# The first weight piece in two halves on two queues, into accumulators set to zero, and the second weight tile requested behind the norm's weights

## The chip, the cores and the metric

The kernel runs on one core of a Trainium2 chip. The metric is the device time of one execution in microseconds (us). The core has a matrix engine (TensorE; PE in the profile, its weight loads PEld), VectorE (DVE), ScalarE (ACT), GpSimd (POOL), SyncE (SP, which mostly issues DMAs here) and 16 DMA engines that serve all queues.

## The reference

One layer of an encoder on 256 positions of width 2048, all in float32. A first norm (RMS norm with the gain `g_mix_pre`) feeds one combined projection `w_in` of 2048 x 5120; attention, a recurrent branch, an output projection, a feed-forward block and a per-layer gate follow. The change touches only the beginning:

```
h = x
hn = rms_norm(h, g_mix_pre[i])
u = hn @ w_in[i]
q, k, v, xr, yg = jnp.split(u, [D_ATTN, 2 * D_ATTN, 3 * D_ATTN, 3 * D_ATTN + D_REC], axis=-1)
```

## The kernel before, in words

Every large product is made of three matmuls. Each float32 operand is split into a high part in the reduced format fp32r (what a cast to it leaves) and a low part (the rest), and the product is high x high + low x high + high x low. The activations are the stationary operand, in blocks of 128 x 128; the weights stream past in 512 columns. A weight tile is 256 rows x 512 columns, kept as two row blocks of 128 x 512 (256 KB each). For each tile a DMA on the SP queue fills a raw buffer `wr` (L611, one of four), ACT casts it to the high part `wh` (L699), VectorE subtracts to make the low part `wl` (L715), and `products` (L730) issues the matmuls: two halves of the positions (t0, t1) x three matmuls x two row blocks, 12 for a tile.

The norm is folded in: the activations are x, transposed, times the gain (`make_hT`, L964): ACT makes the high part `hT_hi` (L330), VectorE the low part `hT_lo` (L332). The gain's 8 KB, `g_first`, are the one load on the ACT queue (L303). The blocks of x come as `xs` (L946) on the SP queue, in between the weights. The scale by row is applied to the result later.

The first three tiles are loaded, cast and subtracted in two pieces of one row block each (`pieces`, L569, with `EARLY`). For tile 0 `products` has an order of its own: first the four matmuls that need the high part alone (L741, L742), then the two with the low part (L755). All later tiles go half by half of the positions through L753, L754 and L755. The first matmul into an accumulator carries a start flag and overwrites it; the others add.

Tiles 0 and 1 take the same rows of `w_in` for two column chunks with two accumulators each; tiles 2 and 3 take the next rows for the same chunks, and so on. On SP the order at the start is: x block 0, tile 0 first piece, x block 1, tile 0 second piece, tile 1 first piece, tile 1 second piece, x blocks 2 and 3, tile 2 in two pieces, tile 3, x blocks 4 and 5. Tile 4 needs the raw buffer of tile 0, so its request waits until VectorE has made the last low part of tile 0.

Before the first segment the program issues a copy on ACT that brings in its function table (L2251) and a warm-up of TensorE: `WARM` = 9 matmuls of a 128x128 float32 tile of ones, two instructions each in the trace (L2254).

The order of the work on ACT, VectorE and SP is not written by hand. A planner (`Plan`) keeps a clock for each engine, with costs written in the code (`act`, `dve`, `dma`; `MM` = 0.2263 for one matmul of 512 columns, `SEM` = 0.15 for a handover), and issues the next operation whose start plus lateness is least, before TensorE's clock reaches it (`plan.run`). `plan.main` advances TensorE's clock for the matmuls. In microseconds of the planner, `dve(n)` is 0.08 + 0.00104 n. For tile 0's first piece the planner counts:

```
plan.main(4 * MM, ev_hi[p], lhs.ev[kx + j])
...
plan.main(2 * MM, ev_lo[p])
```

Of the kernel before, what the change touches and what calls it, by code (L numbers as in the profile page):

```python
# [16 lines left out]
P = 128  # L17
# [71 lines left out]
ADDED = 6.0  # L89
AHEAD = 5  # L90
ISSUE = 160
WARM = 9


class Event:
# [141 lines left out]
def act(n, tables=COPY, take=None, give=None):  # L237
    return ("act", COST["act"] + 0.00082 * n, tables, take, give)
# [15 lines left out]
def layer(ctx: ExitStack, tc: tile.TileContext, a: dict, out: bass.AP):  # L254
# [7 lines left out]
    def f32(t):  # L262
        return t.bitcast(F32)
# [6 lines left out]
    def raw_tile(i):  # L270
        if i not in more_raws:
            return wp.tile([P, 2, N], F32, tag="wr", name="wr", bufs=R_BUFS)
        return t2["third"]
# [4 lines left out]
    def w_kind(i):  # L278
        return f"w{more_w[i]}" if i in more_w else "w"

    def w_tiles(i):
        if i not in more_w:
            return [wp.tile([P, 2, N], F32R, tag=t, name=t) for t in ("wh", "wl")]
        if "w" not in t2:
            t2["w"] = t2["pool"].tile([P, 4, N], F32R, tag="gain", name="w")
        return t2["w"][:, 0:2, :], t2["w"][:, 2:4, :]
# [14 lines left out]

    g_first = const.tile([P, KD], F32, name="g_first")
    nc.scalar.dma_start(g_first, a["vecs"][:, 0:KD])  # L303
    vec = const.tile([P, NVEC], F32, name="vec")
    ident = const.tile([P, P], F32, name="ident")
    make_identity(nc, ident)
# [94 lines left out]
    def done(event):  # L401
        event.t = plan.now
# [170 lines left out]
    def load_stream():  # L573
        for i, tl in enumerate(tiles):
            at_load[0] = i
            if tl is None:
                continue
            w, k, n0 = tl
            if min(fours) <= i < i_ple:
                if i in lower:  # L580
                    yield (ev_spilled, ev_half_spilled, ev_unmerged)[(0, 0, 1, 2, 2)[lower[i]]]
                yield dma(ISSUE, take=raw_kind(i))
                t = lower_tile(lower[i]) if i in lower else raw_tile(i)
                nc.sync.dma_start(t, a[w][n0 // N, k // 2])
                plan.now += COST["landing"]
                if i in ev_load:
                    loaded[i] = t
                    done(ev_load[i])
                else:
                    raws[i] = t  # L590
                    done(ev_raw[i, 2])
                continue
            if i in ev_load:
                first = i in ends_with
                j = ends_with[i if first else i - 1]
                if not first and j:
                    yield ev_big
                yield dma(512, take=raw_kind(i) if first else None)
                loaded[i] = raw_tile(i) if first else last_blocks(3)[:, 0:2, :] if j else t2["third"]
                nc.sync.dma_start(loaded[i], a[w][n0 // N, k // 2])  # L600
                done(ev_load[i])
                continue
            for j in pieces(i):
                for kb, f in extra_loads.get((i, j.start), ()):
                    yield dma(kb)
                    f()
                n = j.stop - j.start
                yield dma(256 * n, take=None if j.start else raw_kind(i))
                if not j.start:
                    raws[i] = raw_tile(i)  # L610
                nc.sync.dma_start(raws[i][:, j, :], a[w][n0 // N, k // 2][:, j, :])  # L611
                done(ev_raw[i, j.stop])

    at_load, at_hi, at_lo, at_pe = [0], [0], [0], [0]
# [67 lines left out]
    def hi_stream():  # L682
        for i in range(len(tiles)):
            at_hi[0] = i
            for j in pieces(i):
                n = j.stop - j.start
                yield ev_raw[i, j.stop]
                if i in big_w:
                    yield big_w[i][2]
                if more_w and i == min(more_w):  # L690
                    for e in mix.chunks:
                        yield e
                yield act(n * N, take=None if j.start or i in big_w else w_kind(i))
                if i in big_w:
                    his[i], los[i] = big_w[i][0](), big_w[i][1]()
                elif not j.start:
                    his[i], los[i] = w_tiles(i)
                src = raws[i] if n == 2 else raws[i][:, j, :]
                nc.scalar.copy(his[i][:, 0 : src.shape[1], :] if n == 2 else his[i][:, j, :], src)  # L699
                done(ev_hi[i, j.stop])  # L700
# [4 lines left out]
    def lo_stream():  # L705
        last_one = max(f[1] for f in ffn_fours().values())
        for i in range(len(tiles)):
            at_lo[0] = i
            for j in pieces(i):
                n = j.stop - j.start  # L710
                yield ev_hi[i, j.stop]
                src = raws[i] if n == 2 else raws[i][:, j, :]
                m = slice(j.start, j.start + src.shape[1])
                yield dve(src.shape[1] * N, give=gives.get(i) or raw_kind(i) if j.stop == 2 else None)
                nc.vector.tensor_tensor(  # L715
                    out=los[i][:, m, :], in0=src, in1=f32(his[i][:, m, :]), op=ALU.subtract
                )
                done(ev_lo[i, j.stop])
            raws.pop(i)
            if i == last_one:  # L720
                done(ev_ple)
            if i == half_end:
                plan.add(reload_half(), plan.now + 22.0)
            if i in fours:
                plan.add(last_sum(i), plan.now, -2 * SOON)
# [4 lines left out]
    def products(i, kx, lhs, accs, ts, start, stop, *after, seeded=False):  # L730
        group = {"skip_group_check": seeded}
        for j in range(2):
            p = (i, j + 1) if (i, j + 1) in ev_lo else (i, 2)
            plan.reach(lhs.ev[kx + j])
            hi, lo = lhs.at[kx + j]
            st, sp = start and j == 0, stop and j == 1
            if i == 0:
                plan.main(4 * MM, ev_hi[p], lhs.ev[kx + j])
                for t in ts:
                    sl = slice(t * P, (t + 1) * P)  # L740
                    nc.tensor.matmul(accs[t], hi[:, sl], his[i][:, j, :], start=st, stop=False, **group)  # L741
                    nc.tensor.matmul(accs[t], lo[:, sl], his[i][:, j, :], start=False, stop=False, **group)  # L742
                plan.main(2 * MM, ev_lo[p])
            else:
                plan.main(6 * MM / NT, ev_lo[p], lhs.ev[kx + j], *after)
            for n, t in enumerate(ts):
                if i and n:
                    if lhs in pT and i > max(ffn_fours()):
                        plan.run()
                    plan.main(6 * MM / NT)  # L750
                sl = slice(t * P, (t + 1) * P)
                if i:
                    nc.tensor.matmul(accs[t], hi[:, sl], his[i][:, j, :], start=st, stop=False, **group)  # L753
                    nc.tensor.matmul(accs[t], lo[:, sl], his[i][:, j, :], start=False, stop=False, **group)  # L754
                nc.tensor.matmul(accs[t], hi[:, sl], los[i][:, j, :], start=False, stop=sp, **group)  # L755
            at_pe[0] = max(at_pe[0], i)
            if j:
                free_w(i)
            plan.run()
# [144 lines left out]
            plan.add(next_gain(("ffn", "g_ffn_post"), plan.clk["pe"]), plan.clk["pe"])  # L904

    keep = set()
    def run_seg(s):
        if callable(s[0]):
            s[0](*s[1:])
            return  # L910
        chunk, lhs, ks, first, last, after, i0 = s
        if after:
            after()
        if first:
            chunk.open()
        for n, (_, kx) in enumerate(ks):
            i = i0 + n
            before = [chunk.ready] if first and n == 0 else [chunk.made] if chunk.made else []
            products(i, kx, lhs, chunk.accs, range(NT), first and n == 0,
                     last and n == len(ks) - 1, *before, seeded=bool(chunk.made))  # L920
            his.pop(i), los.pop(i)
        if last:
            if chunk.before:
                chunk.before()
            plan.add(chunk.post(chunk), plan.clk["pe"] + plan.SEM, chunk.late)
            plan.run()
# [1264 lines left out]
    for i in range(len(tiles)):  # L2191
        for j in pieces(i):
            for ev in (ev_raw, ev_hi, ev_lo):
                ev[i, j.stop] = Event()
    n = 0
    for i in range(min(fours), max(f[1] for f in ffn_fours().values())):
        if tiles[i] is not None and i not in lower:
# [155 lines left out]
```

## Time and profile before

| | us |
|---|---|
| median of 3 runs | 1139.77 |
| lowest and highest | 1138.99, 1140.65 |
| the profiled execution's own time | 1141.41 |
| its span (first to last instruction) | 1139.6 |

The profile is of one execution. Its page gives the busy time of each engine; a timeline row gives start, duration, engine, line, operation, output and inputs, shape, count, and in brackets how long the engine had been idle and what ended that. A matmul's duration contains the pipeline behind it, so the pace of matmuls is the distance of their starts (0.23 us for 512 columns), not their duration (0.39 us). The DMA view gives the size of a request and the time from issue to landing; a landing is the end of the slowest part of the transfer.

### The profile page before, as it was taken

The page shows a single profiled execution, that of the slowest core. Times are in us where ns is not written, and L with a number is a line of the kernel's source. Part 1 is how long each engine was busy: PE and PEld are TensorE (multiplying, and loading weights), DVE is VectorE, ACT ScalarE, POOL GpSimd, SP SyncE. Part 2 cuts the span into 40 slices and gives each one's busy share as a digit, 9 for nine tenths or more (in the row PEclk, how much of TensorE's full clock was granted, in tenths as well). Part 3 has the DMA queues.
Part 4 walks back from the last instruction along what each step waited for, and adds up shares of the span by engine and source line. Part 5 has one row for each costly group of instructions (what it writes and reads, how often), then busy time and mean ns, then how long its engine had stood idle before and what let it go on. Part 6 is the DMA issues. An engine that isn't in the chain of part 4 may idle for free.

```text
span 1139.6 us, 15226 instructions
## 1 busy us (share of the span) xinstructions
PE 1129.5 (99%) x5140; PEld 937.4 (82%) x5140; DVE 962.8 (84%) x1250; ACT 741.3 (65%) x994; POOL 154.8 (14%) x245
## 2 busy tenths in 40 slices
PE   9999999999999999999999999999999999999997
PEld 7888888888888788888888888888888888888886
DVE  6768787788468899899998889999999988988886
ACT  6776788976447556566566656666656664676674
POOL 0000000000000032132011033141121223100200
PEclk9999999999999999999999999999999999999999
DMA  8867666565786977787887777887888787877863
GB/s 313 300 193 220 170 187 184 166 200 181 212 299 184 317 258 235 233 254 223 271 294 225 249 215 217 254 264 228 275 276 285 226 248 250 290 227 269 263 194 109
DMA packets 110687, 269.54 MB, mean 237 GB/s; under 512 B 36433, under 2 KB 42577, under 8 KB 109201
## 3 DMA queue, kind: packets, MB, share of 16 engines
q1 hardware_dynamic: 95568, 242.60, 63.6%
q0 software_dynamic: 14752, 25.84, 11.3%
q8 instruction: 40, 0.66, 0.2%
q14 instruction: 39, 0.31, 0.1%
q10 hardware_dynamic: 288, 0.14, 0.0%
HBM read 250.70 MB, written 9.44 MB: 228 GB/s over the span
## 4 chain that ended last, share of the span: by engine, by line
PE 96%; DVE 2%; ACT 1%; issue 0%; DMA 0%; SPq 0%; DVEq 0%; POOL 0%; ACTq 0%; POOLq 0%
PE acc L755 23%; PE acc L753 23%; PE acc L754 23%; PE acc L766 7%; PE acc L765 7%; PE acc L764 7%; PE tr L343 1%; DVE wl L715 1%; DMA sq<-ev 0%; PE half L2068 0%; PE acc L2068 0%; PE warm L2254 0%; PE pg L390 0%; PE pg L391 0%; PE pg L392 0%
## 5 line engine op out<-in xcount | busy, mean ns | idle before, releaser
L715 DVE TENSOR_TENSOR wl<-wr,wh 128x1024 fp32r<-128x1024 f32 (+1 forms) x295 | 352.7, 1209 | 78.8 <-ACT wh L699 74.6
L699 ACT CAST wh<-wr 128x1024 fp32r<-128x1024 f32 (+1 forms) x295 | 305.3, 1044 | 145.8 <-PE acc L754 83.4
L753 PE MATMUL acc<-wh,hT_mix_hi 128*128 128x512 f32 x376 | 146.6, 390 | 0.0
L754 PE MATMUL acc<-wh,hT_mix_lo 128*128 128x512 f32 x376 | 146.4, 389 | 0.0
L755 PE MATMUL acc<-wl,hT_mix_hi 128*128 128x512 f32 x376 | 146.3, 389 | 0.0
L699 ACT CAST wh<-ple 128x1024 fp32r<-128x1024 f32 (+1 forms) x75 | 76.1, 1019 | 84.8 <-DVE ple L642 54.6
L362 POOL DMA_DIRECT2D mT<-mid x164 | 97.0, 635 | 232.3 <-DVE mid L352 95.6
L755 PE MATMUL acc<-wl,hT_hi 128*128 128x512 f32 x320 | 124.9, 391 | 0.0
L753 PE MATMUL acc<-wh,hT_hi 128*128 128x512 f32 x316 | 124.6, 394 | 0.0
L754 PE MATMUL acc<-wh,hT_lo 128*128 128x512 f32 x316 | 123.2, 390 | 0.0
L668 POOL DMA_DIRECT2D ple<-in_w_ffn_up x32 | 28.7, 897 | 544.8 <-DVE ple L642 388.5
L715 DVE TENSOR_TENSOR wl<-ple,wh 128x1024 fp32r<-128x1024 f32 (+1 forms) x75 | 87.9, 1177 | 9.5 <-ACT wh L699 9.5
L754 PEld LDWEIGHTS acc<-wh,hT_mix_lo 128*128 128x128 f32 x376 | 70.6, 188 | 14.9 <-DVE hT_mix_lo L332 0.3
L755 PEld LDWEIGHTS acc<-wl,hT_mix_hi 128*128 128x128 f32 x376 | 70.6, 188 | 14.8
L753 PEld LDWEIGHTS acc<-wh,hT_mix_hi 128*128 128x128 f32 x376 | 70.6, 188 | 14.7 <-ACT hT_mix_hi L330 0.2
L755 PEld LDWEIGHTS acc<-wl,hT_hi 128*128 128x128 f32 x320 | 60.1, 188 | 13.8 <-DVE wl L715 0.9
L754 PEld LDWEIGHTS acc<-wh,hT_lo 128*128 128x128 f32 x316 | 59.4, 188 | 11.7
L753 PEld LDWEIGHTS acc<-wh,hT_hi 128*128 128x128 f32 x316 | 59.4, 188 | 11.3
L715 DVE TENSOR_TENSOR wl<-lower,wh 128x1024 fp32r<-128x1024 f32 x35 | 42.3, 1213 | 2.4 <-ACT wh L699 2.4
L699 ACT CAST wh<-lower 128x1024 fp32r<-128x1024 f32 x35 | 36.6, 1051 | 10.5 <-PE acc L754 6.7
L753 PE MATMUL acc<-wh,hT_ffn_hi 128*128 128x512 f32 x96 | 37.7, 393 | 0.2 <-ACT hT_ffn_hi L330 0.2
L715 DVE TENSOR_TENSOR wl<-third,wh 128x1024 fp32r<-128x1024 f32 x29 | 35.4, 1220 | 2.6 <-ACT wh L699 2.4
(477 smaller groups left out, 2559.6 us busy)
## 6 DMA issues: line engine op xcount, KB each, us to landing
wr<-in_w_in SPq DMA_DIRECT2D x77, 512.0 KB, 4.5
wr<-in_w_ffn_gate SPq DMA_DIRECT2D x70, 512.0 KB, 5.5
wr<-in_w_ffn_down SPq DMA_DIRECT2D x54, 512.0 KB, 6.0
wr<-in_w_ffn_up SPq DMA_DIRECT2D x50, 512.0 KB, 4.9
wr<-in_w_out SPq DMA_DIRECT2D x32, 512.0 KB, 4.3
wr<-in_w_ple_gate SPq DMA_DIRECT2D x30, 512.0 KB, 5.0
lower<-in_w_ffn_up SPq DMA_DIRECT2D x27, 512.0 KB, 5.7
third<-in_w_ffn_gate SPq DMA_DIRECT2D x18, 512.0 KB, 5.5
```

The lines of the kernel that those rows point to most:

```text
L343: nc.tensor.transpose(tr[:, b, t * P : (t + 1) * P], e[:, t, sl], ident)
L362: (nc.gpsimd if i in pool else nc.sync).dma_start(dst[32 * j : 32 * j + 32, :, :, i, :], src[32 * i : 32 * i + 32, :, :, j, :],)
L668: nc.gpsimd.dma_start(dst, src, accum_op=ALU.add)
L699: nc.scalar.copy(his[i][:, 0 : src.shape[1], :] if n == 2 else his[i][:, j, :], src)
L715: nc.vector.tensor_tensor(out=los[i][:, m, :], in0=src, in1=f32(his[i][:, m, :]), op=ALU.subtract)
L753: nc.tensor.matmul(accs[t], hi[:, sl], his[i][:, j, :], start=st, stop=False, **group)
L754: nc.tensor.matmul(accs[t], lo[:, sl], his[i][:, j, :], start=False, stop=False, **group)
L755: nc.tensor.matmul(accs[t], hi[:, sl], los[i][:, j, :], start=False, stop=sp, **group)
L764: nc.tensor.matmul(dst, x[0], wh, start=start, stop=False, skip_group_check=seeded)
L765: nc.tensor.matmul(dst, x[1], wh, start=False, stop=False, skip_group_check=seeded)
L766: nc.tensor.matmul(dst, x[0], wl, start=False, stop=stop, skip_group_check=seeded)
```

## The change

Six things are changed. `WARM` goes from 9 to 6. Tile 0's first piece is loaded in two halves of 256 columns: the first half by the ACT queue, right behind `g_first`, the second by the SP queue, where the whole piece was. The cast and the subtraction of that piece are two instructions each, of 256 columns. Its matmuls are twelve of 256 columns instead of six of 512: for each half first high x high and low x high for both halves of the positions, then high x low. For these the two accumulators of the first chunk are set to zero by VectorE beforehand, and no matmul of that chunk carries a start flag. And ahead of the request for tile 1's first piece VectorE copies one column of `g_first` into tile 1's raw buffer, so that the request (and what stands behind it on SP) waits until `g_first` has landed.

```
-WARM = 9
+WARM = 6
...
     nc.scalar.dma_start(g_first, a["vecs"][:, 0:KD])
+    first_raw = raw_tile(0)
+    first_w = a["w_in"][3 * DA // N, 0][:, 0, :]
+    nc.scalar.dma_start(first_raw[:, 0, 0:S], first_w[:, 0:S])
...
-                    raws[i] = raw_tile(i)
-                nc.sync.dma_start(raws[i][:, j, :], a[w][n0 // N, k // 2][:, j, :])
+                    raws[i] = raw_tile(i) if i else first_raw
+                if i + j.start == 0:
+                    nc.sync.dma_start(first_raw[:, 0, S:N], first_w[:, S:N])
+                else:
+                    if (i, j.start) == (1, 0):
+                        nc.vector.tensor_copy(out=raws[i][:, 0, 0:1], in_=g_first[:, 0:1])
+                    nc.sync.dma_start(raws[i][:, j, :], a[w][n0 // N, k // 2][:, j, :])
...
+                if i + j.start == 0:
+                    yield act(N, take="w")
+                    his[0], los[0] = w_tiles(0)
+                    nc.scalar.copy(his[0][:, 0, 0:S], first_raw[:, 0, 0:S])
+                    nc.scalar.copy(his[0][:, 0, S:N], first_raw[:, 0, S:N])
...
+                    yield dve(N)
+                    for h in range(2):
+                        cs = slice(h * S, (h + 1) * S)
+                        nc.vector.tensor_tensor(
+                            out=los[0][:, 0, cs], in0=first_raw[:, 0, cs], in1=f32(his[0][:, 0, cs]), op=ALU.subtract
+                        )
...
+            if i + j == 0:
+                for h in range(2):
+                    cs = slice(h * S, (h + 1) * S)
+                    plan.main(2 * MM, ev_hi[0, h], lhs.ev[kx])
+                    for x, w, e in ((hi, his, None), (lo, his, None), (hi, los, ev_lo[0, h])):
+                        if e:
+                            plan.main(MM, e)
+                        for t in ts:
+                            nc.tensor.matmul(
+                                accs[t][:, cs], x[:, t * P : (t + 1) * P], w[0][:, 0, cs],
+                                start=False, stop=False, skip_group_check=True,
+                            )
+                plan.run()
+                continue
...
+        if i0 == 0:
+            zeroed.append(chunk)
+            for acc in chunk.accs:
+                nc.vector.memset(acc, 0.0)
...
-            products(i, kx, lhs, chunk.accs, range(NT), first and n == 0,
-                     last and n == len(ks) - 1, *before, seeded=bool(chunk.made))
+            products(i, kx, lhs, chunk.accs, range(NT), first and n == 0 and i > 0,
+                     last and n == len(ks) - 1, *before, seeded=bool(chunk.made) or chunk is zeroed[0])
```

More of the change, by code (lines that the diff above doesn't have):

```diff
@@ L692, in hi_stream @@
                         yield e
+                if i + j.start == 0:
[3 more added lines that the diff above has]
+                    nc.scalar.copy(his[0][:, 0, S:N], first_raw[:, 0, S:N])
+                    done(ev_hi[0, 0])
+                    done(ev_hi[0, 1])
+                    continue
                 yield act(n * N, take=None if j.start or i in big_w else w_kind(i))
@@ L710, in lo_stream @@
                 n = j.stop - j.start
+                if i + j.start == 0:
+                    yield ev_hi[0, 1]
+                    yield dve(N)
[4 more added lines that the diff above has]
+                        )
+                        done(ev_lo[0, h])
+                    continue
                 yield ev_hi[i, j.stop]
@@ L736, in products @@
             st, sp = start and j == 0, stop and j == 1
+            if i + j == 0:
[11 more added lines that the diff above has]
+                plan.run()
+                continue
             if i == 0:
@@ L906, in layer @@
     keep = set()
+    zeroed = []
     def run_seg(s):
@@ L2194, in layer @@
                 ev[i, j.stop] = Event()
+    ev_hi[0, 0], ev_lo[0, 0] = Event(), Event()
     n = 0
```

## The prediction

> **What bounds the kernel now.** I read the page's head first, then TensorE's busy time in stretches past the start, because the change touches only the start.
>
> ```profile
> span 1139.6 us, 15226 instructions
> PE 1129.5 (99%) x5140; PEld 937.4 (82%) x5140; DVE 962.8 (84%) x1250; ACT 741.3 (65%) x994; POOL 154.8 (14%) x245
> ```
>
> ```profile
> 20.00:120.00 100.00, 100.00 (x468) 1.00 0.77 245
> 120.00:400.00 280.00, 278.87 (x1326) 1.00 0.68 211
> 400.00:1120.00 720.00, 719.79 (x3186) 1.00 0.79 247
> ```
>
> The columns of the second fence are the stretch, its length, TensorE's busy time with its matmuls, the granted clock, the DMA share and GB/s. Between 20 and 1120 us TensorE is idle for 1.35 us of 1100 (0 + 1.13 + 0.21). So the kernel is a chain of matmuls, and whatever the start gains or loses moves the end by the same amount, if the matmuls are already back to back when they leave the start. Where that happens is the question; the timeline of the first 20 us answers it.
>
> ```profile
> 1.14 4.21 PE L2254 MATMUL warm<-ones 128*128 128x128 f32 x18 [1.14 <-POOL ones L308]
> 3.17 0.51 ACT L330 ACTIVATE hT_hi<-xs,g_first 128x256 fp32r<-128x256 f32 x1 [0.50 <-DMA g_first<-in_vecs]
> 3.71 0.48 DVE L332 SCALAR_TENSOR_TENSOR hT_lo<-xs,g_first,hT_hi 128x256 fp32r<-128x256 f32 x1 [3.71 <-ACT hT_hi L330]
> 4.20 0.62 ACT L699 CAST wh<-wr 128x512 fp32r<-128x512 f32 x1 [0.52 <-DMA wr<-in_w_in]
> 4.85 0.69 DVE L715 TENSOR_TENSOR wl<-wr,wh 128x512 fp32r<-128x512 f32 x1 [0.65 <-ACT wh L699]
> 5.00 0.70 PE L741 MATMUL acc<-wh,hT_hi 128*128 128x512 f32 x1
> 5.54 0.40 PE L742 MATMUL acc<-wh,hT_lo 128*128 128x512 f32 x1
> 6.01 0.62 ACT L699 CAST wh<-wr 128x512 fp32r<-128x512 f32 x1 [0.79 <-DMA wr<-in_w_in]
> 6.70 0.48 PE L741 MATMUL acc<-wh,hT_hi 128*128 128x512 f32 x1
> 7.96 0.69 DVE L715 TENSOR_TENSOR wl<-wr,wh 128x512 fp32r<-128x512 f32 x1 [0.60 <-ACT wh L699]
> 8.71 0.51 PE L755 MATMUL acc<-wl,hT_hi 128*128 128x512 f32 x1
> 13.08 1.23 DVE L715 TENSOR_TENSOR wl<-wr,wh 128x1024 fp32r<-128x1024 f32 x1 [1.06 <-ACT wh L699]
> 14.01 1.05 ACT L699 CAST wh<-wr 128x1024 fp32r<-128x1024 f32 x1 [0.55 <-PE acc L755]
> 14.36 0.50 PE L755 MATMUL acc<-wl,hT_hi 128*128 128x512 f32 x1
> 15.91 1.22 DVE L715 TENSOR_TENSOR wl<-wr,wh 128x1024 fp32r<-128x1024 f32 x1
> 17.21 0.46 PE L755 MATMUL acc<-wl,hT_hi 128*128 128x512 f32 x1
> 17.84 2.35 DVE L715 TENSOR_TENSOR wl<-wr,wh 128x1024 fp32r<-128x1024 f32 x2
> ```
>
> Read it in pairs, an operand's end beside the matmul that uses it. Tile 0's second piece: cast ends 6.63 (6.01 + 0.62), matmul 6.70. Tile 1's first low half: 8.65, matmul 8.71. Tile 3's: 14.31, matmul 14.36. Tile 4's: 17.13, matmul 17.21. Four times the matmul starts 0.05 to 0.08 us behind its operand: the weights arrive just in time and have no slack. After tile 4 the lead opens: tiles 5 and 6 are finished by 20.19, while TensorE is still at tile 5. So 17.21 is the last point that fixes the chain. The waits between engines in the first 20 us agree: TensorE's are small, and they are on exactly these operands.
>
> ```profile
> PEld acc L755 <- DVE wl L715: 0.9, 3, 0.3
> PEld acc L741 <- ACT wh L699: 0.3, 1, 0.3
> ```
>
> **Behind the operands stands the DMA queue.** These are the DMA share and GB/s (the last two columns) in three stretches, and then four requests with KB and us to landing, from the DMA view of short windows: the norm's weights (0.74), tile 0's first piece (1.19), tile 1's first piece (2.60), tile 4 (7.39).
>
> ```profile
> 2.00:4.00 2.00, 2.00 (x11) 1.00 0.97 277
> 4.00:8.00 4.00, 4.00 (x19) 1.00 0.85 266
> 8.00:13.00 5.00, 5.00 (x23) 1.00 1.04 408
> ```
>
> ```profile
> g_first<-in_vecs ACTq DMA_DIRECT2D x1, 8.0 KB, 2.4
> wr<-in_w_in SPq DMA_DIRECT2D x1, 256.0 KB, 3.0
> wr<-in_w_in SPq DMA_DIRECT2D x1, 256.0 KB, 4.7
> wr<-in_w_in SPq DMA_DIRECT2D x1, 512.0 KB, 6.5
> ```
>
> From 2 to 13 us the DMA engines are full or nearly so. Tile 4 is asked for at 7.39 and lands at 13.9, and its cast starts at 14.01, so that cast waits for the landing (the releaser named there, L755, read tile 0 long before). An operand's end is therefore set by how many bytes stand ahead of it, not by TensorE.
>
> **The change, part by part.** The prices, from the nearest rows:
>
> ```profile
> 2.12 1.38 SPq L611 DMA_DIRECT2D wr<-in_w_in  x3
> 2.47 0.19 ACT L2251 COPY primed<-eps 128x1 f32<-128x1 f32 x1
> 1102.24 0.37 ACT L2187 COPY half<-acc 128x256 f32<-128x256 f32 x1
> 1129.82 0.15 DVE L2129 TENSOR_TENSOR most<-most,rest 128x1 f32<-128x1 f32 x1
> 1129.89 0.42 DVE L2098 TENSOR_TENSOR mg<-sg,gain_g_ple_post 128x256 f32<-128x256 f32 x1
> 1130.30 0.28 PE L2068 MATMUL half<-wh,hT_ffn_hi 128*128 128x256 f32 x1
> 1130.42 0.28 PE L2068 MATMUL half<-wl,hT_ffn_hi 128*128 128x256 f32 x1
> ```
>
> Warm-up: six of 18 instructions go, at 4.21/18 = 0.23 us, so TensorE is free at 3.9 instead of 5.35. By itself worth nothing before a weight is cast.
>
> First piece in halves: the bytes ahead of the two halves are the same 384 KB (x's first 128 KB, then 256 KB) on the same DMA engines, busy at 0.97. Both halves landing as late as now gives 4.2; the 2.4 us of the small load counted from an issue at 1.6 gives 4.0. I take 4.1, nearer the full queue. The casts take 0.37 each instead of one of 0.62: first half ready at 4.5, second at 4.85; low halves 0.42 each, at 4.95 and 5.35. TensorE starts tile 0 at 4.5 instead of behind the warm-up.
>
> Twelve matmuls of 256 columns replace six of 512: 12 x 0.12 (1130.30 to 1130.42) = 1.44 against 5 x 0.23 = 1.16 from 5.54 to 6.70 plus the first. At up to double that until 5.5 (rivals, below), the piece ends between 6.0 and 6.4. It ended at 6.70. But tile 0's second piece is cast by 6.63. So 0.3 to 0.7 us of the head start turn into waiting for that cast, and 0.07 is left; the next pair (8.65 and 8.71) cuts it to 0.06, tile 3's to 0.05, tile 4's leaves 0.08 at most. **Gain from the head start: 0.05 us.**
>
> Tile 1 behind the norm's weights: the one-element copy on VectorE waits for the 8 KB load (0.74 + 2.4 = 3.14), takes 0.15 and lets SP go on at about 3.35 instead of 2.60: 0.75 us later. Behind it on SP stand tile 1's second piece, x's next blocks, tiles 2 and 3, x again and tile 4. The cover: tile 1's first piece took 4.7 us to land where a load into an empty queue takes 2.4, so it stood in line for 2.3 us, three times the delay; tile 4's request waits for VectorE (7.36), not for SP. Cost with the cover nothing; without it 0.75. The other bound is a gain: fewer bytes compete with tile 0 and the share of 0.85 between 4 and 8 us could fill up, 0.15 x 4 = 0.6 us. I take a gain of 0.1, near the full queue's end, since no byte less stands ahead of tile 4. On VectorE, behind the copy, only L332 at 3.71 waits, 0.4 us after it: nothing, or 0.15 if it came later.
>
> The rest is covered. Two memsets of 128x512 (each at most a subtraction of that size, 0.69) lie in VectorE's idle 3.71 us; uncovered 1.4. The second issue on ACT (1.38/3 = 0.46) moves the copy that ends at 2.66 to 3.12, before L330 at 3.17; uncovered 0.46. One more small DMA on each side of the queue costs no bytes.
>
> The planner's own clock: the split has it wait for a low half after two matmuls' time, so its TensorE clock stands at low half ready (0.612 + 0.15 after the cast) + 0.226 + 0.679 = 1.667 after the cast's release, where it stood at max(0.905, 0.762) + 0.453 = 1.358. This 0.31 us (constants of the code, no time of the chip) can swap work on ACT and VectorE later on. What that can win is bounded by the 1.35 us of idle time; I take zero and keep 1.0 either way.
>
> **Sum.** 0.05 + 0.1 = 0.15 us less. Against the profiled execution, 1141.41 us (span 1139.6 plus 1.8 around it), that is 1141.3; the runs' median of 1139.77 lies 1.6 below that execution, so for a median 1139.6.
>
> **Rivals.** *Slower: the shorter warm-up leaves TensorE slow.* One row speaks for it:
>
> ```profile
> 48.14 0.60 PE L343 MATMUL tr<-ident,ev 128*128 128x128 f32 x4
> ```
>
> Matmuls of the warm-up's shape take 0.60/4 = 0.15 us at most here, but 0.23 at the start, and the first weight matmul, too, holds the array until 5.54. So TensorE runs at about half pace until then, 4.4 us after its first matmul, although the granted clock column shows 1.00. After the change 2.8 us of warm-up are followed by 0.6 us of idle. If that gap starts the count anew at 4.5, full pace comes at 8.9. By then 4.4 us at half pace have done 2.2 us of matmuls, where the kernel before has done 0.23 + (8.9 - 5.54) less 0.1 of waits, 3.5: 1.3 us behind, of which the waits at tiles 3 and 4 give back 0.1: 1139.8 + 1.2 = 1141.0. It decides if full pace comes after about 6.3, where both sides of that count are equal. Against it: the gap is short, and 0.6 idle in 4.4 may not count.
> The Trainium skill, page "TensorE: Matmul & The Clock Gate", speaks against the change: Part 1 has the half clock end after about 3.4 us of sustained matmuls in a window that runs freely, and "Why this matters for your kernels" asks for at least 4 us of warm-up. By the rule, full pace could come a window later, an estimated 3.4 x 0.5 = 1.7 us. The trace fits with its 4.4 us; it cannot show how much idle time a window forgives.
>
> *Faster: the landings move.* If the delayed tile lets tile 0 through and the queue fills its 0.85, tiles 3 and 4 land up to 0.6 us sooner and the head start counts: 1139.77 - 0.7 = 1139.1.
>
> *The planner's order* gets worse by up to 1.0: 1140.7. *The halves land no sooner than the whole:* 4.2 instead of 4.1, which the later waits hide: 1139.7, as forecast.
>
> **How the numbers follow.** Forecast (with the halves that bring nothing) 0.63, half pace 0.13, landings 0.14, planner worse 0.10. The forecast alone, with the 1.7 us by which the three runs differ, spans 1138.9 to 1140.4. The range reaches to the faster case less half of that spread (0.8), 1138.3, and to the half-pace case with 0.2 for its rounding, 1141.2. A measurement tells about 0.2%, 2.3 us, from no change. No single case reaches that; half pace together with a worse order (1.2 + 1.0) almost does, as do sooner landings with a better order and some more: faster 0.02, same 0.94, slower 0.04.
>
> **What would show it.** Right: warm-up over by 4.0, first weight matmul at 4.4 to 4.7, then a longer wait of TensorE for the cast of tile 0's second piece, tile 4's low half done within 0.3 us of 17.13, and the chain dense behind it. Wrong: tile 4 landing over 0.5 us from 13.9; matmuls of 512 columns spaced by over 0.4 us after 6; new idle time between 120 and 400 us.

## The result and the profile after

The median after the change is 1141.24 us (22 runs, 1139.23 to 1142.33), against 1139.40 for the kernel before on the same chip (22 runs, 1138.84 to 1140.72): a ratio of 1.0014, interval 1.0008 to 1.0020. In means, with standard errors, the change costs 1.63 ± 0.21 us. The forecast was 1139.6, and the range ended at 1141.2. So the change is a little slower: under the 0.2% that I called telling, but outside the range and clearly not nothing.

The two profiled executions say the opposite: 1141.41 us before, 1139.23 after. Each is one execution: the first lies above all 22 later runs of its kernel, the second is the lowest of its own 22. The heads of the page after, and TensorE's busy time in the same three stretches (columns as in the prediction):

```profile
span 1137.4 us, 15237 instructions
PE 1127.6 (99%) x5140; PEld 936.5 (82%) x5140; DVE 964.0 (85%) x1254; ACT 740.1 (65%) x995; POOL 154.4 (14%) x245
```

```profile
20.00:120.00 100.00, 100.00 (x468) 83.67 (x467) 72.42 (x112) 75.44 (x111) 0.00 (x0) 1.00 0.77 245
120.00:400.00 280.00, 279.91 (x1335) 233.95 (x1334) 219.49 (x342) 195.35 (x319) 1.85 (x2) 1.00 0.69 214
400.00:1120.00 720.00, 719.72 (x3186) 595.57 (x3186) 649.37 (x760) 448.69 (x531) 150.94 (x228) 1.00 0.79 246
```

Between 120 and 400 us TensorE is idle for 0.09 us here, where the profile before showed 1.13. That is where the two profiles part (a matmul's busy time contains the pipeline behind it, so waits show shorter here than they are; from matmul to matmul, below, it is all of the 2.2 us), and it is not the change's doing, as other executions will show. Each kernel must be judged by its runs; the profiles say only where time can go.

The start of the kernel after, from the timeline of the first 20 us:

```profile
1.14 2.93 PE L2300 MATMUL warm<-ones 128*128 128x128 f32 x12 [1.14 <-POOL ones L311]
3.35 0.15 DVE L618 COPY wr<-g_first 128x1 f32<-128x1 f32 x1 [1.40 <-DMA g_first<-in_vecs]
4.07 0.41 ACT L704 CAST wh<-wr 128x256 fp32r<-128x256 f32 x1 [0.21 <-DMA wr<-in_w_in]
4.53 0.50 PE L771 MATMUL acc<-wh,hT_hi 128*128 128x256 f32 x2 [0.47 <-ACT wh L704]
5.41 0.62 ACT L715 CAST wh<-wr 128x512 fp32r<-128x512 f32 x1 [0.18 <-DMA wr<-in_w_in]
6.08 0.50 PE L781 MATMUL acc<-wh,hT_hi 128*128 128x512 f32 x1
10.31 0.40 PE L795 MATMUL acc<-wl,hT_hi 128*128 128x512 f32 x1
13.99 1.05 ACT L715 CAST wh<-wr 128x1024 fp32r<-128x1024 f32 x1 [0.51 <-DMA wr<-in_w_in]
14.38 0.50 PE L795 MATMUL acc<-wl,hT_hi 128*128 128x512 f32 x1
15.88 1.22 DVE L741 TENSOR_TENSOR wl<-wr,wh 128x1024 fp32r<-128x1024 f32 x1
17.28 0.40 PE L795 MATMUL acc<-wl,hT_hi 128*128 128x512 f32 x1
20.04 0.39 PE L795 MATMUL acc<-wl,hT_hi 128*128 128x512 f32 x1
```

The warm-up ends at 4.07 and the weights start at 4.53, as forecast. Tile 0's second piece starts at 6.08 instead of 6.70, so TensorE is 0.6 us ahead, and it still is at 10.31 (the same matmul before: 10.89). At 14.38 it is level with before (14.36), at 20.04 too (20.03). Its weight loads show where the lead went:

```profile
10.49 0.19 PEld L793 LDWEIGHTS acc<-wh,hT_hi 128*128 128x128 f32 x1 [0.22 <-ACT wh L715]
11.22 0.19 PEld L795 LDWEIGHTS acc<-wl,hT_hi 128*128 128x128 f32 x1 [0.43 <-DVE wl L741]
14.37 0.19 PEld L795 LDWEIGHTS acc<-wl,hT_hi 128*128 128x128 f32 x1 [0.57 <-DVE wl L741]
17.15 0.19 PEld L795 LDWEIGHTS acc<-wl,hT_hi 128*128 128x128 f32 x1 [0.15 <-DVE wl L741]
```

Three waits for tiles 2 and 3, a small one for tile 4, and the head start is gone. What feeds these tiles is the DMA queue, again in DMA share and GB/s (last two columns), followed by the requests for tile 0's first half and tile 4 with KB and us to landing:

```profile
2.00:4.00 2.00, 2.00 (x10) 1.77 (x9) 0.26 (x2) 1.65 (x3) 0.22 (x1) 1.00 0.90 267
4.00:8.00 4.00, 3.54 (x21) 2.92 (x20) 2.95 (x6) 3.02 (x6) 0.00 (x0) 1.00 0.93 284
8.00:13.00 5.00, 5.00 (x21) 3.58 (x21) 2.97 (x6) 3.03 (x6) 0.00 (x0) 1.00 0.95 344
```

```profile
wr<-in_w_in ACTq DMA_DIRECT2D x1, 128.0 KB, 2.9
wr<-in_w_in SPq DMA_DIRECT2D x1, 512.0 KB, 7.1
```

From 8 to 13 us the queue moves 344 GB/s, where it moved 408 before. Tile 4 takes 7.1 us to land instead of 6.5; but it is asked for at 6.82 instead of 7.39, so that in this profile it lands at 13.89, as before (13.91). In the three later profiles of the change it lands at 14.18, 14.39 and 14.92.

Two measures serve for all that follows. The span is about 1.8 us shorter than the time of the execution. **T20** is the start of the matmul that stands at 20.03 in the profile before (the 5060th from the end): what the start lost or won. **The rest** is the span less T20. In the profile after the rest is 1137.45 − 20.04 = 1117.41 us; in the one before 1139.60 − 20.03 = 1119.57.

### The profile page after: what moved, and what is told of

Its sections match the earlier page's. It is cut to its first block, busy times and chain, and to the rows that moved or that the text cites. A ratio compares the mean times of both kernels' runs of the same rounds, so it can differ in the third digit from the quotient of the medians.

```text
span 1137.4 us, 15237 instructions
## 1 busy us (share of the span) xinstructions
PE 1127.6 (99%) x5140; PEld 936.5 (82%) x5140; DVE 964.0 (85%) x1254; ACT 740.1 (65%) x995; POOL 154.4 (14%) x245
## 4 chain that ended last, share of the span: by engine, by line
PE 94%; DVE 2%; DMA 2%; ACT 1%; issue 1%; SPq 0%; DVEq 0%; ACTq 0%
PE acc L793 23%; PE acc L795 23%; PE acc L794 23%; PE acc L806 7%; PE acc L804 7%; PE acc L805 7%; PE tr L346 1%; DMA wr<-in_w_in 1%; DVE wl L741 1%; ACT wh L715 0%; DVE hT_mix_lo L335 0%; DMA lower<-in_w_ffn_up 0%; PE half L2113 0%; PE acc L2113 0%; DMA wr<-in_w_ffn_up 0%
## 5 line engine op out<-in xcount | busy, mean ns | idle before, releaser
L794 PE MATMUL acc<-wh,hT_ffn_lo 128*128 128x512 f32 x96 | 37.5, 390 | 0.0
```

## The experiments

Theory A: half pace after the short warm-up. B: the planner's new order; B2: that order only together with the halves. C: the held-back requests bring later weights late. D: waits after 20 us that scatter from one execution to the next. Mean differences are against runs of the kernel before on the same chip, with standard errors; 11 runs of each kernel unless said otherwise.

**The change again**, on another chip.

> The changed kernel once more, for a second profile beside runs of the kernel before on the same chip. Theory A (the short warm-up and the idle time behind it keep TensorE at half pace for longer, in most executions): about 1.6 us slower than before, 1141.0; its profile shows matmuls of 512 columns 0.43 us apart until some time after 6 us, unless it catches the same early release as the first profile, where the matmuls ran 0.12 us apart (256 columns) from 4.5 on. Theory B (the planner's shifted clock has moved work on ACT and VectorE, and the loss lies in waits of TensorE after 20 us): also 1141.0, but full pace from 5.5 and over 1 us more idle time between 20 and 1120 us. Theory C (the held-back requests of tile 1 and later make weights late in the first 20 us): also 1141.0, with the low half of tile 4 done after 17.6.

Measured: 1140.81 us, ratio 1.0013 (1.0004 to 1.0022), mean +1.30 ± 0.41. Its profile has T20 at 20.33 and a rest of 1118.23. The cost is real, but the signs named for A and C are not in this profile: the clock is at full pace from 4.06 on, and tile 4's low half is done at 17.39. TensorE's waits for operands between 120 and 400 us (us in total, times, longest) show one that the first profile after didn't have:

```profile
PE sc L393 <- DVE pp L329: 0.5, 1, 0.5
```

**The long warm-up back in the change.**

```
-WARM = 6
+WARM = 9
```

> The changed kernel with the warm-up of before (9 matmuls instead of 6), all else as changed. The warm-up then ends at about 5.1, behind the first cast. Theory A: the loss goes, 1139.3 (0.1 us from the kernel before). Theories B and C: it stays, 1141.0.

Measured: 1140.60, ratio 1.0007 (0.9998 to 1.0016), mean +0.75 ± 0.26. That is 0.55 ± 0.46 less than the change on this chip, so a part of the cost may be the warm-up's, but most of it stays.

**The short warm-up alone**: the kernel before with `WARM = 6`.

> The kernel before with 6 warm-up matmuls instead of 9, nothing else. Theory A: slower than before by at least as much as the change, 1.6 to 2.0 us, 1141.0 to 1141.4, since the idle time behind the warm-up is longer here (3.9 to 4.9 us). Theories B and C: nothing of theirs is in it, 1139.4.

Measured: 1140.15, ratio 1.0004 (0.9995 to 1.0013), mean +0.33 ± 0.27, far less than theory A's 1.6 to 2.0. The timeline shows half pace going on much longer than in the change:

```profile
1.14 2.93 PE L2254 MATMUL warm<-ones 128*128 128x128 f32 x12 [1.14 <-POOL ones L308]
4.61 0.79 PE L741 MATMUL acc<-wh,hT_hi 128*128 128x512 f32 x1 [0.55 <-ACT wh L699]
6.05 0.63 PE L742 MATMUL acc<-wh,hT_lo 128*128 128x512 f32 x1
8.19 0.63 PE L741 MATMUL acc<-wh,hT_hi 128*128 128x512 f32 x1
8.61 0.63 PE L742 MATMUL acc<-wh,hT_lo 128*128 128x512 f32 x1
9.75 0.40 PE L753 MATMUL acc<-wh,hT_hi 128*128 128x512 f32 x1
9.98 0.39 PE L754 MATMUL acc<-wh,hT_lo 128*128 128x512 f32 x1
```

From 8.19 to 8.61 a matmul takes 0.42 us, from 9.75 to 9.98 it takes 0.23. So A's mechanism exists. The clock record of the trace goes to full speed at 9.56 us here. In the nine profiles with 12 warm-up matmuls it does so at 4.06, 4.51, 4.78, 5.06, 5.46, 6.95, 8.29, 8.73 and 9.56; in the nine with 16 or more at 4.2 to 5.8, once at 7.30. With a release after 7.2 (three of the nine with the short warm-up, and that one) T20 lies 3.5 to 3.6 us behind the end of tile 4's low part; with an earlier one 2.9 to 3.1 us, the late starts further down left aside. So a late release costs about 0.6 us at 20 us, for the same landing of tile 4. Theory A's mechanism is real and happened in three profiles of nine, about 0.2 us on average; in the four profiles of the change itself it did not happen.

**The change without the held-back requests**, so that tile 1 is requested at once.

```
-                    if (i, j.start) == (1, 0):
-                        nc.vector.tensor_copy(out=raws[i][:, 0, 0:1], in_=g_first[:, 0:1])
```

> The changed kernel without the one-element copy, so that tile 1's first piece is requested right behind tile 0's second piece, as before. Theory A and theory B: no difference to the change, 1141.0. Theory C: back to 1139.4.

Measured: 1140.01, ratio 1.0003 (0.9994 to 1.0012), mean +0.33 ± 0.32, so 1.0 ± 0.5 less than the change on this chip. Tile 4 lands at 13.95 and 399 GB/s flow between 8 and 13 us, as in the kernel before.

**The held-back requests alone**: those two lines added to the kernel before.

> The kernel before with the one-element copy added, so that the requests from tile 1 on wait for the norm's weights; nothing else. Theory A (half pace after the short warm-up): no difference to before, within 0.3 us. Theory B (the planner's shifted order): no difference. Theory C (the held-back requests): slower by 0.7 to 1.2 us, as the first runs of the change with and without the copy differ.

Measured: 1139.96, ratio 1.0000 (0.9991 to 1.0009), mean +0.25 ± 0.17. The 0.7 to 1.2 that theory C expected are not there, although T20 in the profile is 20.61. The DMA queue from 8 to 13 us, in this kernel and then in the next one, which has the halves and no copy:

```profile
8.00:13.00 5.00, 4.79 (x19) 2.96 (x18) 3.34 (x6) 2.98 (x6) 0.00 (x0) 1.00 1.00 372
```

```profile
8.00:13.00 5.00, 5.00 (x23) 4.12 (x22) 3.64 (x7) 3.78 (x7) 0.00 (x0) 1.00 1.02 404
```

372 GB/s with the copy, 404 without. Over all 18 profiles the two groups hardly touch: 344 to 380 GB/s, mean 366, in the ten with the copy; 378 to 408, mean 396, in the eight without. Tile 4 lands at 14.26 on average with it (13.85 to 14.92) and at 13.81 without (13.42 to 14.37). The same holds within each kernel: 14.23 (nine profiles) against 13.69 (three) in the variants of the change, 14.49 (one) against 13.88 (five) in those of the kernel before. The sizes fit: 30 GB/s for 5 us are 0.15 MB, and at 366 GB/s these take 0.4 us; why the queue moves less is not shown. Tile 4's own request is not late, it goes out 0.5 us sooner with the copy (7.01 against 7.54 on average). The loss is there before it: tile 2's second piece lands at 10.98 against 10.56, tile 3 at 12.27 against 11.86. And the landing is what T20 follows: in eleven of the 18 profiles T20 stands 6.1 to 6.2 us behind tile 4's landing; the others are the four with a late release, the two late starts further down and one at 6.3. Theory C stands for the start, 0.45 ± 0.17 us later; for the time of the whole kernel it is not shown at that size.

**The halves and zeroed accumulators alone** (long warm-up, no copy, new order).

```
-WARM = 6
+WARM = 9
...
-                    if (i, j.start) == (1, 0):
-                        nc.vector.tensor_copy(out=raws[i][:, 0, 0:1], in_=g_first[:, 0:1])
```

> The changed kernel with 9 warm-up matmuls and without the one-element copy: the halves, the zeroed accumulators and the planner's shifted order are left. Theory A: as before, within 0.3 us. Theory B: slower than before by as much as the change, 1.3 to 1.6 us. Theory C: as before, within 0.3 us.

Measured: 1140.60, ratio 1.0004 (0.9995 to 1.0013), mean +0.80 ± 0.28. This I had not expected from a part that brings tile 4 at 13.52 and has T20 at 19.84, sooner than before. The profile of its start does not show a loss.

**The change with the planner's old count**, so with the old order of ACT and VectorE.

```
+                plan.main(4 * MM, ev_hi[p], lhs.ev[kx + j])
+                plan.main(2 * MM, ev_lo[p])
...
-                    plan.main(2 * MM, ev_hi[0, h], lhs.ev[kx])
-                    for x, w, e in ((hi, his, None), (lo, his, None), (hi, los, ev_lo[0, h])):
-                        if e:
-                            plan.main(MM, e)
+                    for x, w in ((hi, his), (lo, his), (hi, los)):
```

> The changed kernel, but the planner counts tile 0's first piece as before, so that ACT and VectorE keep the order of before (besides the added instructions). Theory A and theory C: as the change, 1.3 to 1.6 us slower than before. Theory B: as before, within 0.3 us.

Measured: 1139.96, ratio 0.9998 (0.9989 to 1.0007), mean +0.18 ± 0.15. With it alone the order looked like the culprit, so the opposite was run: **the planner's new count in the kernel before.**

```
-                plan.main(4 * MM, ev_hi[p], lhs.ev[kx + j])
+                if j:
+                    plan.main(4 * MM, ev_hi[p], lhs.ev[kx + j])
+                else:
+                    plan.main(2 * MM, ev_hi[p], lhs.ev[kx])
+                    plan.main(MM, ev_lo[p])
+                    plan.main(MM)
```

> The kernel before, but the planner counts tile 0's first piece as in the change, so that ACT and VectorE have the order of the changed kernel; no instruction is added. Theory A and theory C: as before, within 0.3 us. Theory B: 1.3 to 1.6 us slower than before.

Measured: 1139.76, ratio 0.9998 (0.9989 to 1.0007), mean +0.10 ± 0.20. The order by itself has no cost that can be told. What was left was B2, with four kernels on another chip.

**The change a third time.**

> The changed kernel once more, beside the same kernel with the planner's old count on one chip. Theory B2 (the planner's order costs time only together with the halves): 1.3 to 1.6 us slower than before. Theory A (half pace): 0.7 to 1.1 us slower in those executions whose release comes late, and a profile that shows it has the matmul after tile 6 near 20.9 us instead of 20.0. Theory D (nothing but scatter in waits after 20 us, which moves every median by some tenths): within 0.5 us of before.

Measured: 1139.99 (1139.30 to 1142.55), ratio 1.0005 (0.9995 to 1.0014), mean +0.83 ± 0.33. Its profile is of its longest execution, and worth reading for that: T20 is 20.51, the rest 1120.26. The two longest of TensorE's waits between 120 and 400 us and the timeline rows behind them, at the places where the profile before had its own 0.4 and 0.5:

```profile
PE acc L806 <- DVE wl L741: 0.5, 1, 0.5
PE sc L393 <- DVE pp L329: 0.5, 1, 0.5
```

```profile
204.91 0.34 PE L393 MATMUL sc<-kh,qh 128*128 128x160 f32 x1 [0.51 <-DVE pp L329]
391.37 0.50 PE L806 MATMUL acc<-wl,at_hi 128*128 128x512 f32 x1 [0.53 <-DVE wl L741]
```

The same, in the kernel before:

```profile
204.04 0.34 PE L390 MATMUL sc<-kh,qh 128*128 128x160 f32 x1 [0.44 <-DVE pp L326]
390.20 0.50 PE L766 MATMUL acc<-wl,at_hi 128*128 128x512 f32 x1 [0.53 <-DVE wl L715]
```

So these waits belong to neither kernel: some executions of both have them, others do not. The one at 390 us can be followed back to a single slow transfer, a weight tile asked for some 26 us earlier: us to landing (last column) and ScalarE's cast of that tile in the profile before, the same in this one, and the landing in the first profile after, where the cast had no wait:

```profile
wr<-in_w_ffn_up SPq DMA_DIRECT2D x1, 512.0 KB, 7.0
371.06 1.05 ACT L699 CAST wh<-wr 128x1024 fp32r<-128x1024 f32 x1 [1.24 <-DMA wr<-in_w_ffn_up]
wr<-in_w_ffn_up SPq DMA_DIRECT2D x1, 512.0 KB, 7.5
372.38 1.05 ACT L715 CAST wh<-wr 128x1024 fp32r<-128x1024 f32 x1 [1.56 <-DMA wr<-in_w_ffn_up]
wr<-in_w_ffn_up SPq DMA_DIRECT2D x1, 512.0 KB, 5.2
```

In the other 16 profiles this tile takes 4.6 to 6.5 us and the cast waits 0.3 us at most. In these two the work on ScalarE and VectorE behind it runs some 1.4 to 1.7 us later against TensorE, up to the subtraction that TensorE waits for. What makes the transfer slow is not shown. Cut into three stretches, the rest of all 18 profiles reads: from T20 to the matmul 4000 from the end, 215.56 to 216.78 us; from there to the one 3000 from the end, 223.14 to 223.55, apart from the profile before (224.61) and this one (224.82); from there to the end, 678.57 to 678.87, but 679.93 once. The three lowest sum to 1117.3, and seven of the 18 profiles lie within 0.5 us of that. The span of an execution is therefore T20, plus 1117.4, plus the waits that it happens to meet: none, or up to 2.9 us. Theory D's scatter is seen; that it is all of the difference is not, since the mean of the change lies above that of the kernel before in all its sets of runs.

**The old order a second time, on that chip.**

> The changed kernel with the planner's old count, for the second time, on the same chip as the changed kernel itself. Theory B2: within 0.3 us of before and 1 us or more faster than the changed kernel. Theory A: as the changed kernel. Theory D: within 0.5 us of the changed kernel.

Measured: 1139.82, ratio 1.0005 (0.9996 to 1.0014), mean +0.53 ± 0.28. One execution of 2951.82 us, which nothing in the kernel explains, is left out of the mean. The difference to the change is 0.30 ± 0.40: unclear.

**The halves alone with the old order** (no copy, long warm-up, and the planner's old count).

> The halves and the zeroed accumulators alone, with 9 warm-up matmuls, without the one-element copy and with the planner's old count. Theory B2: within 0.3 us of before, where the same kernel with the new count was 0.8 us slower. Theory A: within 0.3 us of before. Theory D: within 0.5 us of before.

Measured: 1140.10, ratio 1.0004 (0.9996 to 1.0013), mean +0.51 ± 0.20, against +0.80 ± 0.28 with the new order on another chip. No difference to be told.

**The change with 16 warm-up matmuls**, `WARM = 8`.

> The changed kernel with 8 warm-up matmuls instead of 6. The warm-up then ends at 4.7, where the first half is cast, so that no idle time is left and TensorE starts the weights without loss. Theory A: the loss is gone, within 0.3 us of before, and the profile's release comes before 7.3 us. Theory B2: as the change, 1.3 to 1.6 us slower. Theory D: within 0.5 us of before.

Measured: 1140.14, ratio 1.0004 (0.9995 to 1.0012), mean +0.56 ± 0.20, 0.27 ± 0.36 less than the change on this chip.

By then no part alone had cost more than 0.8, and the profiles of the change (T20 at 20.04, 20.33, 20.51) stood only some 0.3 to 0.45 us behind those of the kernel before (20.03, and 19.67 with the new order). Whether such a loss reaches the end at all, as my first premise had it, had never been measured. The next two kernels delay the start of the kernel before by a known amount and change nothing else.

**A late start alone**: `WARM = 15` in the kernel before.

> The kernel before with 30 warm-up matmuls in place of 18, nothing else: a late start and no other part of the change. The row "48.14 0.60" puts a matmul of the warm-up's shape at about 0.12 to 0.15 us at full pace, so TensorE is free 1.4 to 1.8 us later, and with some 0.35 us of waits between 5 and 17 us to absorb it the matmul that stood at 20.03 us should stand at 21.1 to 21.5. Theory E, my prediction's own premise (what the start loses moves the end by the same amount): mean +1.1 to +1.5 us against the kernel before. Theory F (waits after 20 us, for weights that land between 180 and 390 us, are there anyway and give a late start back): +0.5 or less.

Measured: 1141.73, ratio 1.0017 (1.0008 to 1.0026), mean +2.01 ± 0.34.

**A later start**: `WARM = 24`.

> The kernel before with 48 warm-up matmuls in place of 18: 30 more at 0.12 to 0.15 us, so TensorE is free 3.6 to 4.5 us later and the matmul that stood at 20.03 us should stand at 23.3 to 24.2. Theory E (a start loss goes through to the end): mean +3.3 to +4.2 us. Theory F (later waits give it back): at most +2, since the waits after 20 us that the traces show sum to 1.35 us in the slowest profile of the kernel before, so no more than about 1.4 us can be given back by them and +2 to +2.8 would be the least that is left; a value below +2 would need other slack.

Measured: 1142.37 (7 runs), ratio 1.0027 (1.0017 to 1.0038), mean +3.01 ± 0.36. The warm-up, the first weight matmul and the matmul of T20, in the kernel with 30 and then in the one with 48:

```profile
1.14 5.67 PE L2254 MATMUL warm<-ones 128*128 128x128 f32 x30 [1.14 <-POOL ones L308]
6.56 0.48 PE L741 MATMUL acc<-wh,hT_hi 128*128 128x512 f32 x1
...
20.77 0.39 PE L755 MATMUL acc<-wl,hT_hi 128*128 128x512 f32 x1
```

```profile
1.14 7.06 PE L2254 MATMUL warm<-ones 128*128 128x128 f32 x48 [1.14 <-POOL ones L308]
7.95 0.48 PE L741 MATMUL acc<-wh,hT_hi 128*128 128x512 f32 x1
...
22.13 0.39 PE L755 MATMUL acc<-wl,hT_hi 128*128 128x512 f32 x1
```

T20 is 0.74 and 2.10 us later than in the profile before: less than expected, since 18 more warm-up matmuls at full pace took 7.95 − 6.56 = 1.39 us, 0.08 each. The time grew by 2.0 and 3.0. Theory F (given back) falls: at least what the start loses arrives at the end. But theory E, a loss of the same amount, falls short too: in both cases about 1 us more came on top (2.01 − 0.74 = 1.3 and 3.01 − 2.10 = 0.9, each ± 0.35 and with T20 from one execution). The profiled executions do not have it (rests of 1117.62 and 1117.60, near the least), but they are among the fastest of their kernels, 1140.17 and 1141.52; others took up to 1143.12 and 1144.19. Whether those had a later T20 or more waits behind it was not profiled. The spread is wider too: the standard deviation of single runs is 0.54 us for the kernel before on this chip and 1.08 and 0.93 for these two.

**The change a fourth time, on the chip of the late starts.**

> The change itself on a fourth chip, as the mark for the next kernel. Means so far +1.63, +1.30 and +0.83 us against the kernel before; their mean +1.25. If the start alone were the cause (theory E with the 0.45 us by which the profiles of the change stand later at 20 us): +0.45.

Measured: 1140.29, ratio 1.0009 (1.0000 to 1.0018), mean +1.05 ± 0.28. T20 is 21.03, the latest of the four, with a rest of 1117.45. ScalarE's cast of tile 4 and TensorE's wait for its low part:

```profile
15.02 1.05 ACT L715 CAST wh<-wr 128x1024 fp32r<-128x1024 f32 x1 [0.89 <-DMA wr<-in_w_in]
```

```profile
18.18 0.50 PE L795 MATMUL acc<-wl,hT_hi 128*128 128x512 f32 x1 [0.29 <-DVE wl L741]
```

Tile 4 lands at 14.92 here, one whole microsecond later than before, and the matmul that stood at 17.21 stands at 18.18. Nothing behind it gives that back: T20 is 1.0 late.

**The old order a third time.**

> The change with the planner's old count of tile 0's first piece, so the old order of a dozen casts and subtractions in the first 20 us; the work is the same. Theory B2 (the new order costs, together with the halves): +0.3 us against the kernel before, as the two runs so far (+0.18 and +0.53), and 0.5 to 1.0 below the change on this chip. If the order is worth nothing: the same as the change on this chip, within 0.4.

Measured: 1139.99, ratio 1.0008 (0.9999 to 1.0017), mean +0.85 ± 0.26, 0.20 ± 0.35 below the change. The expected gap of 0.5 to 1.0 is not there. On the two chips where they ran side by side the old order won 0.30 and 0.20, together 0.24 ± 0.27. B2 is not shown: at two errors (0.78) the order would have a good half of the cost, and it may have nothing of it.

## Why the prediction was wrong

Taken over all four sets of runs (55 of the change), the change costs 1.3 us: the forecast of no change that the 0.2% can tell holds in size, but its sum of −0.15 had the wrong sign, and the range was too short on the slow side. Two steps failed as far as the runs show: the term of the held-back requests, taken as a gain of 0.1, and the term for all that comes after 20 us, taken as zero. The first is explained at 20 us; how the second arises stays open.

**Right: the base. Half right: the premise.** The profile's own 1141.41 was taken to lie 1.6 above the median; the stretches now say why (its waits at 204 and 390 us). That what the start loses moves the end was right in direction. "By the same amount" was not shown: the late starts cost about 1 us more than their T20, and the copy alone, with T20 0.6 later in its profile, cost 0.25 ± 0.17. Two slips in the arithmetic do not matter: 0, 1.13 and 0.21 sum to 1.34, not 1.35, and a spread of 1.7 around 1139.6 goes from 1138.75 to 1140.45.

**Right at 20 us: the head start brings nothing, though not where I put it.** Casts, warm-up, zeroing and the second issue on ScalarE cost about what was worked out: the first weight matmul at 4.53 for a forecast of 4.5. But in the first profile no wait stood ahead of tile 0's second piece. That piece also came sooner, and the lead of 0.6 us lasted until tile 2, at 10.5. In the three other profiles of the change the piece starts at 6.18, 6.44 and 6.52, a smaller lead, and at tile 1's first low half (8.71 before) it is −0.09, 0.06 and 0.24. In the time of the whole kernel the halves do not come out as nothing: alone they cost 0.51 ± 0.20 and, with the new order, 0.80 ± 0.28, for a forecast gain of 0.05.

**Wrong: the term of the held-back requests.** "Cost with the cover nothing; without it 0.75 ... I take a gain of 0.1." Measured: a cost of 0.45 ± 0.17 at tile 4's landing. The cover (tile 1's first piece stands in line for 2.3 us anyway) holds for tile 1 itself, which lands no later. It does not hold for the stream behind it: with everything on SP up to tile 3 asked for 0.6 to 0.7 us later on average, the queue ran 8% slower between 8 and 13 us, and from tile 2's second piece on all came some 0.4 us late; tiles 3 and 4 had under 0.1 us of slack, and paid. I had the slack of each operand in the table of pairs and checked the cover at tile 1 alone. Of the other bound (sooner landings) only the first part came true: tile 0's second piece did land sooner, which brought nothing. In the time of the whole kernel this term is less certain: the copy alone cost 0.25 ± 0.17, taking it out of the change won 0.98 ± 0.50.

**Half right: half pace.** The rival's mechanism is real, in 3 of 9 profiles with the short warm-up, but priced twice too high: 0.6 us, not 1.2, since a slower TensorE also waits less for tiles 2 to 4 (in the profile of the change without the copy, with its release at 8.73, it does not wait for them at all). The rule of the Trainium skill that spoke against the change (page "TensorE: Matmul & The Clock Gate", "Why this matters for your kernels": at least 4 us of warm-up) names the right danger. The trace agrees as far as it goes: late releases in three of nine profiles with 2.9 us of warm-up, in one of nine with more; so few do not show the difference.

**Wrong: nothing after 20 us.** "I take zero and keep 1.0 either way" was meant for the planner's order, and for the order alone zero was right (+0.10 ± 0.20). But I read the idle 1.35 us of the profile as a bound on what order can win. It was a sample of waits that come and go. Of the change's 1.3 us, T20 accounts for 0.45 (mean 20.48 ± 0.21 in its four profiles, against 20.03), or 0.6 with the kernel before and its new order averaged as the base. The remaining 0.7 to 0.85 are a subtraction. That they lie in waits after 20 us is likely, but the profiles do not show it: the rest of the change's four is 1118.3 on average, that of the kernel before and its new order 1119.0. The late starts point the same way, with about 1 us more than T20 says from a pure delay of 0.7 and 2.1 us, and leave the same gap, since only their fast executions were profiled.

**The parts add up.** Each alone against the kernel before: the copy 0.25, the short warm-up 0.33, the new order 0.10, the halves 0.51, in sum 1.2 ± 0.4. That is the 1.3 of the change, so no cost of parts acting together, as in B2, is needed; the halves are the largest, and none of the four is known well enough to be called the culprit.

**Open.** Why nearly all variants of the start take longer than their T20 accounts for is not settled. The wait at 390 us goes back to one slow transfer; whether a start shifted by half a microsecond makes such transfers more frequent was not seen. That the halves alone cost 0.5 to 0.8, with T20 at 19.84 in one profile and 20.26, behind a late release, in the other, belongs to the same question. Since profiles are of single executions, the share of each place in the mean could not be measured.

## What to carry to other kernels

Where several operands in a row arrive with under 0.1 us of slack, check a held-back request against the last of them, not against the next one: here the next one landed in time and everything behind it came some 0.4 us late. A profile is one draw: when the bottleneck engine's few idle stretches sum to about what a change is worth, compare them over several executions before calling them a bound. And delaying the start by a known amount is a cheap kernel that tells whether anything lost there arrives at the end.

## What the runs showed of the hardware

- TensorE's clock record goes to full speed between 4.06 and 9.56 us after the first instruction with 12 warm-up matmuls and a gap of 0.5 us behind them, and between 4.2 and 7.3 with 16 to 48. The granted-clock column reads 1.00 ahead of that too, and only the distance of the starts (0.42 against 0.23 us) shows the half pace.
- The DMA engines moved 237 to 306 GB/s with a share of 0.77 to 1.09 in the stretches 2 to 4 and 4 to 8 us, and 344 to 408 at 0.95 to 1.05 from 8 to 13 (18 profiles). Full engines do not mean equal rate.
- The same instructions, in the same order, took from 1117.4 to 1120.3 us after T20 in four profiles of one kernel.
- The same 512 KB weight tile, asked for at the same point of the program some 364 us into it, took 4.6 to 6.5 us to land in 16 profiles and 7.0 and 7.5 in two; those two are the ones in which TensorE waits 0.5 us at 390.
